# The first MLP product of a hybrid encoder step as a seven-product block scheme too

## The chip, the cores and the metric

The kernel runs on one core of a Trainium2 chip. The metric is the device time of one launch in microseconds (us). Shown are the median of three runs and one profiled execution. TensorE (PE) multiplies, VectorE (DVE), ScalarE (ACT) and GpSimd (POOL) do elementwise work, SyncE (SP) issues most of the loads.

## The reference

One step of a two-layer encoder on 1056 tokens (1024 of a prompt, 32 of a running stream) of width 1024, in fp32. Each layer mixes tokens (layer 0 by causal pooling, layer 1 by differential attention, both beside an attention into 256 memory tokens), projects, and runs an MLP of width 4096:

```python
def sq_relu_mlp(x, w1, w2):
    h = jax.nn.relu(x @ w1)
    return (h * h) @ w2
...
        x = x + jnp.concatenate([t_out, m_out], axis=-1) @ w_out[l]
        x = x + sq_relu_mlp(rmsnorm(x, g_ffn[l]), w_ff1[l], w_ff2[l])
    return rmsnorm(x, g_final), ...
```

`rmsnorm` divides a token by the root of its mean square and multiplies by a gain per channel.

## The kernel before

**Data.** Tokens lie in the free dimension, in three groups g0, g1, g2 of 352 (`GW`); channels lie on partitions, in 8 chunks of 128. An fp32 operand is held as two parts, `hi` (a rounded copy, cast by ScalarE) and `lo` (source minus `hi`, on GpSimd or VectorE). `mm3` (lines 44 to 46) makes one fp32 product of three matmuls: hi·hi, hi·lo, lo·hi. `part` (lines 98, 99) splits a weight tile of 512 columns, `split` (lines 49, 50) a tile of 352.

**PSUM.** In the MLP eight banks: four `xb`, two `mm`, two `dn`. A bank is taken again when VectorE has read what was in it.

**Stages.** Layer 0's mixer (to about 234 us), output projection (to 326), MLP (to 1010), layer 1's mixer (to 1411), projection (to 1504), MLP (to 2213), last stores. `tail` is projection and MLP: the projection goes by three sets of output chunks j, each over all three groups; x gets the result added (line 948), its squares are summed (lines 178, 179), `rstd` (lines 188 to 195: a ones matmul, then ScalarE, then VectorE) makes the scale `rs` of each token, and `take` (lines 208, 209) splits x times the gains. The scale itself is multiplied in only after ff1 (line 1104).

**MLP.** The hidden width is worked through in 16 blocks b of 256, which are two chunks of 128. `ff1(b)` makes six results (two chunks by three groups), each a sum over 8 input chunks, 144 matmuls a block; VectorE makes relu(product) times `rs` (line 1104), ScalarE squares (line 1105). `ff2_pair(b)` already takes g0 and g1 through a 2x2 block product with seven products instead of eight: its weights are four blocks A11 to A22 and four sums S1 to S4, its hidden operands B11 to B22 and T1 to T4; g2 runs plainly. That is 44 products of 3 matmuls, and VectorE adds them to x in 40 evictions (lines 1123 `xb`, 1132 `mm` singles, 1144 plain g2). The last two blocks' second product runs plainly in `ff2_last`.

**What sets the order.** `ff1(b+1)` and `ff2_pair(b)` are woven step by step, three matmuls of each in turn. Splits, weight sums (line 1041, VectorE) and hidden differences (line 1080, GpSimd) are jobs with hand-written places in a count of 48 steps a block (`self.job`). A weight sum may be placed no earlier than the eviction that was last when its job came up (`issue_after(self.last_add...)`). Within such limits a scheduler fixes each engine's list at build time; each engine then runs its own list in order and waits on semaphores. Weights come as raw tiles of 512 KB, three in flight; ten hi/lo pairs are held.

Of the kernel before, what the change touches and what calls it, by code (L numbers as in the profile page):

```python
# [29 lines left out]
NW = 10  # L30
NWB = 14
YOFF = 896
# [3 lines left out]
class Kern:  # L36
# [15 lines left out]
    def weights(self):  # L52
# [14 lines left out]
        for l in range(2):  # L67
            if l:
                for h in range(4):
                    yield t["w_kv"][h], GKV, g  # L70
                    yield t["w_kv"][4 + h], GKV, g
                    yield t["w_in"][8 + h], GA + 8, g
                for h in range(4):
                    yield t["w_in"][12 + h], GA + 8, g
            for j in range(8):
                yield t["w_out"][8 * l + j], None, g
            yield from ((t["w_ff1"][32 * l + i], None, g) for i in range(2))
            yield None

    def raw_tile(self):  # L80
        return self.wpool.tile([128, 8, 128], F32, tag="wraw", name="wraw", bufs=3)

    def weight_load(self):
        if self.wstop:
            return
        w = next(self.wlist, None)
        if w is None:
            self.wstop = True
        else:
            raw = self.raw_tile()  # L90
            self.nc.sync.dma_start(raw.rearrange("p a b -> p (a b)"), w[0])
            self.wraw.append((raw,) + w[1:])

    def part(self, src, eng):

        hi = self.wpool.tile([128, 4, 128], F32R, tag="whi", name="whi", bufs=NW)
        lo = self.wpool.tile([128, 4, 128], F32R, tag="wlo", name="wlo", bufs=NW)
# [4 lines left out]
    def weight_split(self):  # L102
# [5 lines left out]
        raw, gcol, eng = self.wraw.pop(0)  # L108
        if gcol is not None:
            g = self.gains[:, gcol:gcol + 8].unsqueeze(2).broadcast_to([128, 8, 128])  # L110
            nc.gpsimd.tensor_tensor(raw, raw, g, ALU.mult)
        self.wready.append([self.part(raw[:, 4 * a:4 * a + 4], eng) for a in range(2)])
# [13 lines left out]

    def g_dense(self, ps, W, g):
        for c in range(C):
# [4 lines left out]
        self.tick()  # L133
# [78 lines left out]
    def setup(self):  # L212
        nc, t, ctx, tc = self.nc, self.t, self.ctx, self.tc
        self.done = set()
        self.pu, self.pend, self.last_exp = {}, [], None
# [4 lines left out]
        self.wpool = ctx.enter_context(tc.tile_pool(name="wpool", bufs=1))  # L220
        self.xpool = ctx.enter_context(tc.tile_pool(name="xpool", bufs=1))
        self.xh, self.xl, self.rs = [None] * NG, [None] * NG, [None] * NG
        self.acc2 = self.xpool.tile([128, GW], F32, name="acc2")
# [12 lines left out]
    def setup_late(self, b, p):  # L236
# [3 lines left out]
        self.dists = b.tile([128, 288], F32, name="dists")  # L240
        nc.sync.dma_start(self.dists, t["dists"])
        for i in range(0, 1152, 384):
            dt = p.tile([128, 384], F32, tag="os", name="dt", bufs=2)
# [4 lines left out]
        lq = b.tile([128, 388], F32, name="lq")  # L248
# [14 lines left out]
    def mem_load(self, p):  # L263
        self.mx = p.tile([128, C, 256], F32, name="memx")
        self.nc.sync.dma_start(self.mx, self.t["mem"])

    def mem_rstd(self, p):
        self.mr = p.tile([128, 256], F32, name="mr")
# [323 lines left out]
    def mix0(self, U):  # L592
        nc, t = self.nc, self.t
        with self.tc.tile_pool(name="att0", bufs=1, reuse_waits="tile") as p:
# [11 lines left out]
            with self.tc.tile_pool(name="mem", bufs=1, reuse_waits="tile") as mp:  # L606
                wr = p.tile([128, 4, 128], F32, tag="pA3", name="wpr", bufs=2)
                self.wph = mp.tile([128, 4, 128], F32R, name="wph")
                self.wpl = mp.tile([128, 4, 128], F32R, name="wpl")
                nc.sync.dma_start(wr, t["w_pool"])  # L610
                self.split(self.wph, self.wpl, wr)
                self.mem_load(mp)
                self.mix0_drive(p, mp, dd, qq, qs, U)
# [39 lines left out]
    def diff_project(self, h, p, out, smp):  # L653
# [3 lines left out]
        for g in range(NG):  # L657
# [83 lines left out]
    def diff_scores(self, h, pair, p, d, A):  # L741
# [4 lines left out]
        for i in (2 * pair, 2 * pair + 1):  # L746
# [4 lines left out]
            for c in range(2):  # L751
# [12 lines left out]
                if c:  # L764
                    pr = self.pd.tile([128, Wk], F32, tag="p1", name="pr", bufs=1)
# [124 lines left out]
    def mix1(self):  # L890
        self.nq, self.nmk = 4, 1
        with self.tc.tile_pool(name="att1", bufs=1, reuse_waits="tile") as p, \
                self.tc.tile_pool(name="attd", bufs=1, reuse_waits="tile") as self.pd, \
                self.tc.tile_pool(name="tabs", bufs=1, reuse_waits="tile") as tabs:
            dd, qq = {}, {}
            self.qp = p
            self.claim(p, (("q", 1024, self.nq), ("qf", GW, 2), ("st", 16, 4), ("pA3", 1024, 2), ("aTh", 512, 2),
                           ("aTl", 512, 2), ("mkr", 256, 1), ("mk", 512, 1), ("mv", 512, 1), ("os", 512, 2),
                           ("rs_y", 256, 1), ("rs_r", 256, 1), ("sq", 256, 1), ("of", 256, 2)))
# [3 lines left out]
            self.claim(self.pd, (("kst", NT, 1), ("vst", NT, 1), ("ks", 2 * SEQ, 1), ("std", 8, 4), ("pA2", 768, 2),  # L903
                                 ("p1", 1024, 1), ("v", 2 * SEQ, 1)))
            self.setup_late(tabs, p)
# [11 lines left out]
    def tail(self, l):  # L917
        nc, t = self.nc, self.t
        with self.tc.tile_pool(name=f"ff{l}", bufs=1, reuse_waits="tile") as p:
            xin = t["xT"] if l == 0 else self.xscr  # L920
            with ExitStack() as st:
                pad = st.enter_context(self.tc.tile_pool(name=f"pad{l}", bufs=1, reuse_waits="tile"))
                self.claim(pad, (("pad", 4000, 1),))
                po = st.enter_context(self.tc.tile_pool(name=f"out{l}", bufs=1, reuse_waits="tile"))
                o = [po.tile([128, 8, GW], F32, name=f"o{g}") for g in range(NG)]
                for cs in (range(7), range(7, 8)):
                    for g in range(NG):
                        for c in cs:
                            nc.sync.dma_start(o[g][:, c, :], self.oscr[l][c][:, g * GW:(g + 1) * GW])
                for g in range(NG):  # L930
                    self.alloc_x(g)
                    for c in range(8):
                        self.take(o[g][:, c, :], g, c)
                x = [p.tile([128, C, GW], F32, name=f"x{g}") for g in range(NG)]
                acc = [p.tile([128, GW], F32, name=f"acc{g}") for g in range(NG - 1)] + [self.acc2]
                self.claim(p, (("sq", GW, 2),))
                for g in range(NG):
                    nc.sync.dma_start(x[g][:, 0:3], xin[g][:, 0:3])
                for g in range(NG):
                    nc.sync.dma_start(x[g][:, 3:8], xin[g][:, 3:8])  # L940
                for js in ((0, 1, 2), (3, 4, 5), (6, 7)):
                    W = {j: self.weight() for j in js}
                    for g in range(NG):
                        for j in js:
                            k = 3 * g + j
                            ps = (self.xtile if js[0] == 0 and 2 <= k < 6 else self.dntile)()[:, :GW]
                            self.dense(ps, W[j], g)
                            nc.vector.tensor_tensor(x[g][:, j, :], x[g][:, j, :], ps, ALU.add)
                            self.sumsq_add(acc[g], x[g][:, j, :], j == 0, p, eng=nc.gpsimd if j < 6 else None)
                        if js[-1] == 7:  # L950
                            self.alloc_x(g)
                            for c in range(8):
                                self.take(x[g][:, c, :], g, c, GF + 8 * l)
                            self.after(1, lambda g=g: self.rstd(acc[g], D, self.new_rs(g)))
            with self.tc.tile_pool(name=f"h2{l}", bufs=1, reuse_waits="tile") as ph:
                self.ff(l, p, ph, x, acc)
# [5 lines left out]
    def ff(self, l, p, ph, x, acc):  # L962
        self.at, self.jobs, self.ph = -48, [], ph
        self.rawlist = [t for b in range(NWB) for t in (("a", b + 1, 0), ("r", b, 0), ("r", b, 1), ("a", b + 1, 1))]
        self.rawlist += [("a", NB - 1, 0), ("a", NB - 1, 1)] + [("r", NWB + i, k) for i in range(2) for k in range(2)]
        self.raws, self.W1, self.W2, self.H = {}, {}, {}, {}
# [4 lines left out]
        for b in range(NWB, NB):  # L971
            self.plan_last(b)
        for b in range(1, NB):
            for i in range(2):
                at = 48 * (b - 1) + (14 if i else -10)
                self.job(at, lambda b=b, i=i: self.first_part(b, i))
        self.jobs.sort(key=lambda x: x[0])
        self.l = l
        self.W1[0] = [self.weight(), self.weight()]
        for _ in range(3):  # L980
            self.next_raw(l)
        for _ in self.ff1(0):
            self.pos()
        for b in range(NWB):
            two = self.ff2_pair(b, x)
            for k, _ in enumerate(self.ff1(b + 1)):
                next(two, None)
                self.pos()
            for _ in two:
                pass  # L990
# [343 lines left out]
```

## Time and profile before

| | us |
|---|---|
| median of three runs (lowest, highest) | 2225.0 (2223.94, 2226.67) |
| profiled execution, its own time | 2226.33 |
| its span | 2224.6 |
| TensorE busy, matmuls | 2162.5, 13521 |
| VectorE / GpSimd / ScalarE busy | 1314.4 / 1174.6 / 913.8 |
| mean granted TensorE clock | 0.988 |

The profile is of one execution. "L1041 DVE" is an instruction of line 1041 on VectorE; `out<-in` are the program's names, then shapes, count, busy time and mean. In a timeline a row gives start, duration, engine, line, and in brackets how long the engine was idle before and what ended that. Several instructions of a kind in a row are put together (x3).

### The profile page before, as it was taken

The numbers are of one execution on the slowest core, as the hardware profiler recorded it, in microseconds if no ns is written. First come the engines' busy times: TensorE is split into PE (matmuls) and PEld (weight loads), VectorE is DVE, ScalarE is ACT, GpSimd is POOL, SyncE is SP. The second block draws the span as 40 slices with busy tenths as digits, with TensorE's granted clock in tenths as the row PEclk, the third lists the DMA queues.
The fourth block names the chain that finished last, engine by engine and source line by source line (L and its number), as shares of the span: only waits on it lengthen the run. The fifth ranks groups of instructions, "written<-read, shape, count | busy, mean of one in ns | idle before, by whom it ended". The sixth has DMA issues, their size and how long they took to land.

```text
span 2224.6 us, 35342 instructions
## 1 busy us (share of the span) xinstructions
PE 2162.5 (97%) x13521; PEld 2120.0 (95%) x13521; DVE 1314.4 (59%) x2466; ACT 913.8 (41%) x1947; POOL 1174.6 (53%) x1096
## 2 busy tenths in 40 slices
PE   6999999999999999999999999999999999999997
PEld 6898999999999999998999988899999999999997
DVE  8855255566566666647566776235666656665635
ACT  5455353333333333334466766344333333333335
POOL 5225336666666666653433223335666666766653
PEclk9999999999999999999999999999999999999999
DMA  5445401111111111223222214411111111211112
GB/s 190 148 134 171 143 29 38 48 58 48 40 47 58 48 48 38 64 61 134 89 72 58 75 53 126 146 37 39 39 48 58 48 46 40 60 46 48 39 48 79
DMA packets 63642, 158.02 MB, mean 71 GB/s; under 512 B 10608, under 2 KB 30320, under 8 KB 62960
## 3 DMA queue, kind: packets, MB, share of 16 engines
q1 hardware_dynamic: 62176, 152.03, 21.7%
q10 hardware_dynamic: 1296, 3.74, 0.5%
q8 instruction: 106, 1.74, 0.3%
q14 instruction: 64, 0.52, 0.1%
HBM read 125.66 MB, written 25.88 MB: 68 GB/s over the span
## 4 chain that ended last, share of the span: by engine, by line
PE 84%; DVE 5%; ACT 4%; issue 1%; DMA 1%; SPq 0%; DVEq 0%; ACTq 0%
PE dn L44 16%; PE dn L45 16%; PE dn L46 16%; PE mm L44 7%; PE mm L45 7%; PE mm L46 7%; PE xb L44 4%; PE xb L46 4%; PE xb L45 4%; DVE xl L50 1%; PE sc L759 1%; PE mm L801 1%; PE sc L761 1%; PE sc L760 1%; DMA o<-oscr 1%
## 5 line engine op out<-in xcount | busy, mean ns | idle before, releaser
L44 PE MATMUL dn<-xh,whi 128*128 128x352 f32 x2408 | 787.7, 327 | 15.8 <-ACT xh L208 7.6
L45 PE MATMUL dn<-xl,whi 128*128 128x352 f32 x2408 | 779.7, 324 | 1.9 <-DVE xl L209 1.9
L46 PE MATMUL dn<-xh,wlo 128*128 128x352 f32 x2408 | 777.9, 323 | 0.0
L99 POOL TENSOR_TENSOR wlo<-wraw,whi 128x512 fp32r<-128x512 f32 x332 | 434.8, 1317 | 483.6 <-ACT whi L98 483.0
L44 PEld LDWEIGHTS dn<-xh,whi 128*128 128x128 f32 x2408 | 455.4, 189 | 20.2 <-ACT xh L208 7.6
L45 PEld LDWEIGHTS dn<-xl,whi 128*128 128x128 f32 x2408 | 456.0, 189 | 6.1 <-DVE xl L209 3.4
L46 PEld LDWEIGHTS dn<-xh,wlo 128*128 128x128 f32 x2408 | 456.2, 189 | 0.3
L98 ACT CAST whi<-wraw 128x512 fp32r<-128x512 f32 x368 | 223.9, 620 | 542.9 <-PE mm L45 256.3
L1123 DVE TENSOR_TENSOR x<-x,xb 128x352 f32<-128x352 f32 x448 | 233.5, 521 | 172.9 <-PE xb L46 172.8
L44 PE MATMUL mm<-h2h,whi 128*128 128x352 f32 x880 | 284.9, 324 | 0.0
L46 PE MATMUL mm<-h2h,wlo 128*128 128x352 f32 x880 | 283.2, 322 | 0.0
L45 PE MATMUL mm<-h2l,whi 128*128 128x352 f32 x880 | 282.7, 321 | 0.0
L1132 DVE TENSOR_TENSOR x<-x,mm 128x352 f32<-128x352 f32 x448 | 222.6, 518 | 85.1 <-PE mm L46 84.9
L50 POOL TENSOR_TENSOR h2l<-hid,h2h 128x352 fp32r<-128x352 f32 x164 | 154.8, 951 | 103.2 <-ACT h2h L49 99.2
L1144 DVE TENSOR_TENSOR x<-x,mm 128x352 f32<-128x352 f32 x224 | 116.3, 519 | 148.9 <-PE mm L46 148.9
L1105 ACT ACTIVATE hid<-hid 128x352 f32<-128x352 f32 x192 | 95.3, 496 | 230.9 <-DVE hid L1104 229.0
L99 POOL TENSOR_TENSOR wlo<-ws,whi 128x512 fp32r<-128x512 f32 x112 | 168.1, 1521 | 37.5 <-ACT whi L98 20.0
L1104 DVE SCALAR_TENSOR_TENSOR hid<-dn,rs 128x352 f32<-128x352 f32 x192 | 100.1, 521 | 132.6 <-PE dn L46 130.8
L45 PEld LDWEIGHTS mm<-h2l,whi 128*128 128x128 f32 x880 | 165.5, 188 | 0.4
L44 PEld LDWEIGHTS mm<-h2h,whi 128*128 128x128 f32 x880 | 165.3, 188 | 0.4
L46 PEld LDWEIGHTS mm<-h2h,wlo 128*128 128x128 f32 x880 | 165.4, 188 | 0.0
L44 PE MATMUL xb<-h2h,whi 128*128 128x352 f32 x448 | 144.5, 322 | 0.0
(243 smaller groups left out, 3416.1 us busy)
## 6 DMA issues: line engine op xcount, KB each, us to landing
wraw<-in_w_ff SPq DMA_DIRECT2D x128, 512.0 KB, 3.6
o<-oscr SPq DMA_DIRECT2D x48, 176.0 KB, 3.6
wraw<-in_w_in SPq DMA_DIRECT2D x16, 512.0 KB, 4.1
wraw<-in_w_mem SPq DMA_DIRECT2D x16, 512.0 KB, 3.8
wraw<-in_w_out SPq DMA_DIRECT2D x16, 512.0 KB, 3.9
x<-in_xT SPq DMA_DIRECT2D x12, 352.0 KB, 7.6
xscr<-x SPq DMA_DIRECT2D x3, 1408.0 KB, 4.7
out_y<-x SPq DMA_DIRECT2D x24, 176.0 KB, 1.8
```

What stands on the lines that cost most here:

```text
L44: mm(ps, lhsT=ah, rhs=bh, start=first, stop=False, skip_group_check=more)
L45: mm(ps, lhsT=ah, rhs=bl, start=False, stop=False, skip_group_check=more)
L46: mm(ps, lhsT=al, rhs=bh, start=False, stop=last, skip_group_check=more)
L50: (lo_eng or self.nc.vector).tensor_tensor(lo, src, hi.bitcast(F32), ALU.subtract)
L98: self.nc.scalar.copy(hi, src)
L99: eng.tensor_tensor(lo, src, hi.bitcast(F32), ALU.subtract)
L759: nc.tensor.matmul(o, lhsT=self.slid[:, h, :], rhs=self.dtab[:, y:y + n], start=True, stop=False)
L1104: nc.vector.scalar_tensor_tensor(h, ps, 0.0, self.rs[g], ALU.max, ALU.mult)
L1105: nc.scalar.activation(h, h, AF.Square)
L1123: add(xj, xj, X[j], ALU.add)
L1132: add(xj, xj, ps, ALU.add)
L1144: self.last_add = add(xj, xj, ps, ALU.add)
```

## The change

The first MLP product of g0 and g1 becomes the same kind of seven-product scheme, block by block: 44 steps of three matmuls instead of 48, 132 matmuls a block instead of 144. Relu needs the finished result, so the scheme's operands must be normalised tokens: x times gain times `rs` is made before (line 1004 of the changed kernel), and from it the operands B11, B21, B22 and T1 to T4 once a layer (`operands0`, `operands1`; g2 in `operands2`), each split into hi and lo. ff1's weights get S1 to S4 in each block too: eight parts a block instead of four, and four more sums on VectorE (line 1148). Partial sums p1, p4, u3 live in freed tiles. Relu and square are two ScalarE instructions (lines 1188, 1189).

In ff2 the splits of its S weights move from GpSimd to VectorE (line 102); its products come in another order and there are 44 evictions (line 1319), since the chain S3·T3 has two targets. ff2 lags ff1 by 66 steps of 44 a block. The output projection keeps six banks open over chunks 0 to 6 and does g2 before chunks j3 to j7 of g0, g1, g2. Raw weight tiles are 256 KB, six in flight; eight hi/lo pairs are held. Groups are finished in the order 2, 0, 1 (`ORDER`), and pools and the tables of layer 1's mixer are set up in another order (`setup_late`).

VectorE in the woven MLP. `mm`, `xb` and `dn` are PSUM banks, `x_2604` to `x_2606` (before) and `x_2657` to `x_2659` (after) the three groups. Before, among the plain products of g2:

```order
L1144 TENSOR_TENSOR x_2606<-x_2606,mm 128x352
L1041 TENSOR_TENSOR ws<-wraw 128x512
L1144 TENSOR_TENSOR x_2606<-x_2606,mm 128x352
L1041 TENSOR_TENSOR ws<-ws,wraw 128x512
L1144 TENSOR_TENSOR x_2606<-x_2606,mm 128x352
L1041 TENSOR_TENSOR ws<-wraw 128x512
L1104 SCALAR_TENSOR_TENSOR hid<-dn,rs_3399 128x352
L1144 TENSOR_TENSOR x_2606<-x_2606,mm 128x352
L1041 TENSOR_TENSOR ws<-wraw,ws 128x512
```

Now, at the end of the plain products of g2 and through the singles A22·T4 (`x_2657`) and S4·B22 (`x_2658`):

```order
L1319 TENSOR_TENSOR x_2659<-x_2659,mm 128x352 x2
L102 TENSOR_TENSOR wlo<-ws,whi 128x512
L1319 TENSOR_TENSOR x_2657<-x_2657,mm 128x352
L1148 TENSOR_TENSOR ws<-wraw 128x512
L1319 TENSOR_TENSOR x_2657<-x_2657,mm 128x352
L1148 TENSOR_TENSOR ws<-ws,wraw 128x512
L1319 TENSOR_TENSOR x_2657<-x_2657,mm 128x352
L1148 TENSOR_TENSOR ws<-wraw 128x512
L1319 TENSOR_TENSOR x_2657<-x_2657,mm 128x352
L1319 TENSOR_TENSOR x_2658<-x_2658,mm 128x352
L1148 TENSOR_TENSOR ws<-wraw,ws 128x512
```

These four sums are those of ff1's weights; ff2's own four still stand among the plain products, further up. In the step from the projection into ff1, VectorE's list now ends thus (T_3391 and T_3392 are T3 and T4, the sums those of block 0, `rs_3690` the scale of g2):

```order
L53 TENSOR_TENSOR T_3391<-xf,T_3391 128x352 x2
L964 TENSOR_TENSOR x_2659<-x_2659,mm 128x352
L1051 TENSOR_TENSOR xf<-xf,t_3487 128x352
L1051 TENSOR_TENSOR xf<-xf,t_3489 128x352
L184 TENSOR_TENSOR acc_2662<-acc_2662,sq 128x352
L53 TENSOR_TENSOR T_3392<-xf,T_3392 128x352 x2
L1148 TENSOR_TENSOR ws<-wraw 128x512
L1258 TENSOR_TENSOR b_3682<-p_3667,dn 128x352
L1148 TENSOR_TENSOR ws<-ws,wraw 128x512
L1148 TENSOR_TENSOR ws<-wraw 128x512
L1148 TENSOR_TENSOR ws<-wraw,ws 128x512
L198 SCALAR_TENSOR_TENSOR rs_3690<-xb,rs_3690 128x352
```

The weight sums of block 0 stand behind the last operand, T4; before, this place held only casts' `lo` parts and the scales. The core of the diff:

```diff
-NW = 10
+NW = 8
+NRAW = 6
+STEPS = 44
+ORDER = (2, 0, 1)
...
-                for js in ((0, 1, 2), (3, 4, 5), (6, 7)):
-                    W = {j: self.weight() for j in js}
-                    for g in range(NG):
-                        for j in js:
...
+        for g in range(2):
+            for j in range(3, 8):
+                ps = self.bank()
+                self.dense(ps, W[j], g)
+                added(g, j, ps)
+            if g == 0:
+                self.after(1, lambda: self.operands0(l, sp, po, x[0], acc[0]))
+        more = self.operands1(l, sp, p, po, x[1], acc[1])
+        for j in range(3, 8):
+            ps = self.bank()
+            self.dense(ps, W[j], 2)
+            added(2, j, ps)
+            next(more, None)
...
+        for c in range(4):
+            b12.append(self.norm(l, 1, x, c, po))
+            v(b11[c], b12[c], b11[c], ALU.subtract)
+            self.put("T1", c, b11[c], c % 2)
...
         for b in range(NB):
-            self.plan_hidden(b)
+            self.plan_weights("a", b, STEPS * b, (("A11", -8), ("A12", -2), ("A21", 8), ("A22", 12), ("S2", 20),
+                                                  ("S3", 24), ("S1", 28), ("S4", 32)))
         for b in range(NWB):
-            self.plan_pair(b)
+            at = STEPS * (b + 1) + 22
+            self.plan_weights("r", b, at, (("A12", -8), ("A11", -4), ("A21", 8), ("A22", 10), ("S4", 20), ("S2", 24),
+                                           ("S1", 28), ("S3", 32)))
...
-            with self.tc.issue_after(self.last_add.ins):
-                nc.vector.tensor_tensor(s, x, y, op)
+            with self.tc.issue_after(self.last_add.ins) if self.last_add else ExitStack():
+                nc.vector.tensor_tensor(S[k], x, y, op)
...
         def part(k):
+            src = S.pop(int(k[1])) if k[0] == "S" else raw(("A11", "A12", "A21", "A22").index(k))
+            self.A[kind, b, k] = self.part(src, nc.vector if k[0] == "S" and kind == "r" else g)
...
+        for k in range(4):
+            self.job(at + 12 + 2 * k, lambda k=k: add(k + 1))
...
+    def ff1(self, b):
+        yield from self.plain(b, 1)
+        yield from self.one(b, "A11", "B11")
+        p1 = self.role("p1")
+        nc.scalar.copy(p1, self.ps)
+        yield from self.one(b, "A12", "B21")
+        h = self.role("B11")
+        add(h, p1, self.ps, ALU.add)
+        self.hidden(b, "B11", h, h)
...
+    def ff1_first(self):
+        yield from self.one(0, "A11", "B11")
...
+        yield from self.one(0, "A12", "B21")
...
+        yield from self.one(0, "S4", "B22")
...
+        yield from self.one(0, "S1", "T1")
...
+        yield from single("A12", "B21", (0, 0))
+        yield from plain(0, "A11", "A12")
+        yield from chain("A11", "B11", (0, 0), first=True)
+        yield from plain(1, "A21", "A22")
+        yield from single("A22", "T4", (0, 1))
+        yield from single("S4", "B22", (1, 0))
+        yield from chain("S2", "T2", (1, 0))
+        yield from single("S1", "T1", (1, 1), (1, 0))
+        yield from chain("S3", "T3", (1, 1), (0, 1))
```

More of the change, by code (lines that the diff above doesn't have):

```diff
@@ L125, in dense, with g_dense @@
             pass
-    def g_dense(self, ps, W, g):
-        for c in range(C):
+    def g_dense(self, ps, W, g, chunks=range(C)):
+        for c in chunks:
             hi, lo = W[c // 4]
@@ L988, in ff @@
+            self.plan_hidden(b, at)
+        self.plan_last(sp)
+        self.jobs.sort(key=lambda x: x[0])
+        third = self.operands2(l, ph, x[2], acc[2])
+        for _ in self.ff1_first():
+            self.pos()
+            if self.at > 8:
+                next(third, None)
+        second = self.second(x)
+        for b in range(1, NB):
+            for _ in self.ff1(b):
                 self.pos()
-            for _ in two:
-                pass
-        for _ in self.ff1(NB - 1):
-            self.pos()
+                if self.at > STEPS + 22:
+                    next(second, None)
@@ L993, in ff @@
+        for _ in second:
+            pass
         while self.jobs:
@@ L995, in ff, with second @@
         self.wstop = False
-        self.ff2_last(l, p, x, acc)
+        self.ff2_last(l, p, x)
+    def second(self, x):
+        for b in range(NWB):
+            yield from self.ff2_pair(b, x)
     def job(self, at, fn):
@@ L1095, in ff1, with raw @@
[L1095 to L1106 removed]
+        def raw(k):
+            return self.raws[kind, b, k]
@@ new lines, in part @@
+        def part(k):
+            src = S.pop(int(k[1])) if k[0] == "S" else raw(("A11", "A12", "A21", "A22").index(k))
+            self.A[kind, b, k] = self.part(src, nc.vector if k[0] == "S" and kind == "r" else g)
+        if kind == "a" and b == 0:
+            part("A11")
+            part("A12")
+            a22 = []
+            for k in (1, 2, 3):
+                add(k)
+            a21 = raw(2), raw(3)
+            add(4)
+            for k in ("S4", "S1", "S2", "S3"):
+                part(k)
+            self.A["a", 0, "A22"] = self.part(a21[1], g)
+            self.A["a", 0, "A21"] = self.part(a21[0], g)
+            return
@@ new lines, in hidden, with steps @@
+    def hidden(self, b, k, src, h=None):
+        h = h or self.role(k)
+        self.nc.scalar.activation(h, src, AF.Relu)
+        self.nc.scalar.activation(h, h, AF.Square)
+        self.H[b][k] = h
+    def steps(self, ps, b, a, x, first=True, last=True):
+        hi, lo = self.A["a", b, a]
+        for c in range(4):
+            if isinstance(x, int):
+                bh, bl = self.xh[2][:, 4 * x + c, :], self.xl[2][:, 4 * x + c, :]
+            else:
+                bh, bl = self.X[x][:, 0, c, :], self.X[x][:, 1, c, :]
+            self.mm3(ps, hi[:, c, :], lo[:, c, :], bh, bl, first and c == 0, last and c == 3)
+            yield
@@ L1130, in single, with plain @@
                 for g, u in to:
-                    xj = x[g][:, j + 4 * u, :]
-                    add(xj, xj, ps, ALU.add)
-        yield from chain("A11", "B11", 0, 0, first=True)
-        yield from single("A12", "B21", (0, 0))
-        for u, a1, a2 in ((0, "A11", "A12"), (1, "A21", "A22")):
+                    add(g, j, u, ps)
+        def plain(u, a1, a2):
             for j in range(4):
@@ L1208, in x_rstd @@
         nc = self.nc
-        acc = [p.tile([128, GW], F32, name=f"acc{g}{i}") for i in range(2)]
+        acc = [p.tile([128, GW], F32, tag=f"acc{i}", name=f"acc{g}{i}", bufs=2) for i in range(2)]
         for c in range(C):
```

506 lines of the change are left out of this document (313 added, 193 removed).

## The prediction

> **What bounds the kernel now.** I read the page first, then the table of windows, then VectorE's and GpSimd's timelines inside one steady stretch of the MLP. From the page, the engines' busy time and the head of the chain of waits:
>
> ```profile
> PE 2162.5 (97%) x13521; PEld 2120.0 (95%) x13521; DVE 1314.4 (59%) x2466; ACT 913.8 (41%) x1947; POOL 1174.6 (53%) x1096
> PE 84%; DVE 5%; ACT 4%; issue 1%; DMA 1%; SPq 0%; DVEq 0%; ACTq 0%
> ```
>
> The windows (per stretch: length, then busy time and instructions of PE, PEld, DVE, ACT, POOL, the granted clock, DMA share, GB/s):
>
> ```profile
> 400.00:900.00 500.00, 500.00 (x3138) 500.00 (x3138) 307.00 (x565) 161.29 (x310) 327.47 (x286) 1.00 0.16 49
> 1580.00:2080.00 500.00, 500.00 (x3139) 500.00 (x3138) 306.93 (x566) 160.44 (x308) 326.81 (x286) 1.00 0.16 50
> 486.00:529.00 43.00, 43.00 (x271) 43.00 (x270) 26.37 (x50) 14.07 (x27) 27.30 (x24) 1.00 0.17 50
> 310.00:330.00 20.00, 19.61 (x118) 18.70 (x117) 17.70 (x33) 15.39 (x34) 5.46 (x4) 1.00 0.00 0
> 1034.00:1064.00 30.00, 23.64 (x118) 23.17 (x119) 22.15 (x34) 10.62 (x24) 16.22 (x16) 0.83 0.43 146
> ```
>
> In both MLPs TensorE is never idle: 500 us for 3138 matmuls, 0.1593 us each, at full clock. The step from the output projection into the MLP (310 to 330) loses only 0.4 us. The whole kernel is TensorE's list of matmuls plus some 60 us of gaps elsewhere; a removed matmul is worth its 0.159 us as long as VectorE (61% busy in the steady stretch) and GpSimd (65%) still answer in time.
>
> **What is removed.** The first MLP product falls from 144 to 132 matmuls in each of 16 blocks and two layers: 16 x 2 x 12 = 384 matmuls, 384 x 0.1593 = **61.2 us**. A woven pair of an ff1 block and an ff2 block falls from 276 matmuls (43.97 us) to 264 (42.06 us), so 28 pairs hold 1.91 x 28 = 53.5 us of it; the rest lies in blocks without a partner.
>
> **What is added in a pair.** VectorE gets four more evictions or sums, four more weight sums (line 1148) and the four `lo` splits of the S weights (line 102). Its durations, from the timelines of VectorE and of GpSimd:
>
> ```profile
> 488.71 0.52 DVE L1144 TENSOR_TENSOR x<-x,mm 128x352 f32<-128x352 f32 x1 [1.37 <-PE mm L46]
> 489.14 1.29 DVE L1041 TENSOR_TENSOR ws<-wraw 128x512 f32<-128x512 f32 x1
> 491.07 0.72 DVE L1041 TENSOR_TENSOR ws<-ws,wraw 128x512 f32<-128x512 f32 x1
> 492.98 1.43 DVE L1041 TENSOR_TENSOR ws<-wraw 128x512 f32<-128x512 f32 x1
> ...
> 495.20 0.92 DVE L1041 TENSOR_TENSOR ws<-wraw,ws 128x512 f32<-128x512 f32 x1
> 498.30 0.52 DVE L1144 TENSOR_TENSOR x<-x,mm 128x352 f32<-128x352 f32 x1 [1.40 <-PE mm L46]
> 500.21 0.52 DVE L1144 TENSOR_TENSOR x<-x,mm 128x352 f32<-128x352 f32 x1 [1.40 <-PE mm L46]
> ...
> 506.90 2.86 DVE L1132 TENSOR_TENSOR x<-x,mm 128x352 f32<-128x352 f32 x6 [0.43 <-PE mm L46]
> ```
> ```profile
> 488.03 1.85 POOL L50 TENSOR_TENSOR h2l<-hid,h2h 128x352 fp32r<-128x352 f32 x2 [2.21 <-ACT h2h L49]
> 489.84 1.40 POOL L50 TENSOR_TENSOR h2l<-hs,h2h 128x352 fp32r<-128x352 f32 x1
> 492.58 4.70 POOL L99 TENSOR_TENSOR wlo<-ws,whi 128x512 fp32r<-128x512 f32 x3 [1.33 <-PE mm L46]
> 497.24 0.95 POOL L1080 TENSOR_TENSOR hs<-hid 128x352 f32<-128x352 f32 x1
> ```
> ```profile
> L1041 DVE TENSOR_TENSOR ws<-wraw 128x512 f32<-128x512 f32 x56 | 76.6, 1367 | 0.0
> L1041 DVE TENSOR_TENSOR ws<-wraw,ws 128x512 f32<-128x512 f32 x28 | 25.9, 925 | 0.0
> L1041 DVE TENSOR_TENSOR ws<-ws,wraw 128x512 f32<-128x512 f32 x28 | 20.5, 731 | 0.0
> L99 DVE TENSOR_TENSOR wlo<-wraw,whi 128x512 fp32r<-128x512 f32 x36 | 26.4, 744 | 16.4 <-ACT whi L98 16.0
> L99 POOL TENSOR_TENSOR wlo<-wraw,whi 128x512 fp32r<-128x512 f32 x332 | 434.8, 1317 | 483.6 <-ACT whi L98 483.0
> L98 ACT CAST whi<-wraw 128x512 fp32r<-128x512 f32 x368 | 223.9, 620 | 542.9 <-PE mm L45 256.3
> ```
>
> An eviction from PSUM takes 0.52 and leaves VectorE free after 0.43 (488.71 to 489.14). A weight sum of the same form takes 0.72 where GpSimd soon falls idle (491.07; GpSimd's split ends at 491.24) and 1.29 or 1.43 where a GpSimd operation is under way (489.14, 492.98). In these rows the sum ends about 0.57 after the GpSimd operation under way does (489.84 to 490.43; 491.24 to 491.79), and the GpSimd operation behind it is stretched (1.40 for one that takes 0.95).
>
> The Trainium skill, page "SBUF — State Buffer", section "Who interferes with whom", has a rule that speaks against this change: a VectorE operation with two SBUF inputs and a GpSimd operation that reads SBUF share a port, and the second to issue waits until the first has ended. The rows agree with it. By the rule, in an unbroken row of GpSimd work, each of the new sums would wait out a GpSimd split less the eviction ahead of it (estimate: 1.29 - 0.44 + 0.57 = 1.42), and the stall below would lie near its upper bound.
>
> *VectorE's load of a pair*: 44 ff2 evictions and 6 ff1 sums at about 0.46 make 23; eight weight sums at 1.10 (mean of the three groups above) 8.8; four splits at 0.74 to 1.3, 3 to 5. Together 35 to 37 of 42.06 us, 85%, where before it was 26.4 of 43. GpSimd has 12 weight splits at 1.3, nine hidden splits, four subtractions and a sum at 0.95: 29 of 42. Both fit on average. The question is where the work stands.
>
> *Its place.* Before, the four sums stand between evictions of the plain products, one every 1.92 us (498.30, 500.21). Now four sums (the r weights) still stand there, but the other four (the a weights) stand between the evictions of the single products A22·T4, one every 6 x 0.1593 = 0.956 us. There are two `mm` banks, so a product takes the bank of the one 1.91 us before it. From TensorE's timeline, one such product:
>
> ```profile
> 506.23 0.32 PE L44 MATMUL mm<-h2h,whi 128*128 128x352 f32 x1
> ...
> 506.55 0.32 PE L46 MATMUL mm<-h2h,wlo 128*128 128x352 f32 x1
> ```
>
> Its eviction starts at 506.90, 0.67 after its start, and takes 0.52; so VectorE may be 0.70 us late, and what is beyond holds TensorE. With the group means in program order: 0.44 + 1.37 - 0.956 = 0.85 late, a stall of 0.15; then 0.44 + 0.73 - 0.956 = 0.21 more, stall 0.21; then 0.85 more, stall 0.85; the fourth sum has an interval without a sum ahead of it and adds nothing. Sum 1.2 us. The S splits stand directly before these singles and between the plain evictions (1.92 apart); at 0.74 they fit, at 1.25 they hand on 0.3 to 1 us. GpSimd's list runs through here without a gap (four subtractions, then weight and hidden splits in turn), so I take **1.6 us a pair**: 28 x 1.6 = 45 us. Bounds: every sum at 0.72 and every split at 0.7, nothing is more than 0.7 late, 0 to 0.25 us, 0 to 7 us in all; every sum at 1.43 (492.98) and the splits at 1.1, three stalls of 0.9 and one of 0.4 from the sums and 1 from the splits, about 4 us, 112 us in all.
>
> **What is added at the step into the MLP** (twice). From VectorE's timeline of the old step and of the kernel's start, GpSimd's at both, and TensorE's after a gap at 228:
>
> ```profile
> 306.64 0.52 DVE L948 TENSOR_TENSOR x<-x,dn 128x352 f32<-128x352 f32 x1 [2.14 <-PE dn L46]
> 308.70 3.06 DVE L209 SCALAR_TENSOR_TENSOR xl<-x,gains,xh 128x352 fp32r<-128x352 f32 x6
> 313.97 0.52 DVE L195 TENSOR_TENSOR rs<-rs,rs_y 128x352 f32<-128x352 f32 x1
> 20.50 8.83 DVE L209 SCALAR_TENSOR_TENSOR xl<-x,gains,xh 128x352 fp32r<-128x352 f32 x8
> ```
> ```profile
> 319.78 5.50 POOL L99 TENSOR_TENSOR wlo<-wraw,whi 128x512 fp32r<-128x512 f32 x4 [18.04 <-ACT whi L98]
> 20.10 1.27 POOL L1218 TENSOR_TENSOR acc<-acc,sqp 128x352 f32<-128x352 f32 x1
> ```
> ```profile
> 228.60 0.50 PE L44 MATMUL dn<-xh,whi 128*128 128x352 f32 x1
> 230.87 0.32 PE L46 MATMUL dn<-xh,wlo 128*128 128x352 f32 x1
> ```
>
> Count from the end of the last projection product of group 1. TensorE then has five products of group 2 (120 matmuls, 19.1 us) and A11·B11, A12·B21 (24, 3.8 us): work until 22.9. Next is S4·B22, and S4 is a weight sum which stands on VectorE behind all of T1 to T4. The scale of group 1 is there 7.8 us after the last eviction (306.64 to 314.49). Then come 34 SBUF operations of 352 columns (8 norms, 10 splits, 12 differences, 4 sums of squares), four evictions, four weight sums. At 0.51 an operation (308.70, GpSimd idle) this is 17.3 + 1.8 + 3.3 = 22.4, done at 30.2; at a third of the way to 1.10 (20.50, GpSimd busy) 24 + 1.8 + 4.5, done at 38. ScalarE's cast (0.62) and GpSimd's `lo` (1.3) follow: the third matmul of S4·B22 can run at 32 to 40. TensorE idles 9 to 17 us, and then runs at the half clock first: 8 matmuls in 2.27 us (228.60 to 230.87) for 1.27, 1 us more. I take 13 each, **26 us** for both; the least is 0 to 4 (if the norms are spread better than their order suggests), the most 34. Cover for the old step was that VectorE needed only casts and `lo` of the tokens, 8 operations a group.
>
> **Smaller terms.** The relu and square (two ScalarE operations a result for one VectorE and one ScalarE) and copies of p1, p4 lie on ScalarE, 33% busy in a pair: nothing. Half-tile loads double the DMA issues on SP but not the bytes, at a share of 0.16: nothing, and 2 us if a queue held them. At the entry of the last ff2 GpSimd has more splits to catch up: 3 us (0 to 6). At the entry of mixer 1, VectorE is held 1.70 us for a table and TensorE idles 6.4 of 30 us:
>
> ```profile
> 1052.37 2.03 DVE L245 CAST dtab<-dt 128x384 fp32r<-128x384 f32 x1 [1.70 <-DMA dt<-in_dtab]
> ```
>
> The table's load now stands ahead of other claims on its pool, and group 2 is finished first; I take 4 us back (0 to 8). The output projection's reordering removes no matmul; its six open banks wait less for the last heads: 0 (2 either way).
>
> **Sum.** The profiled execution took 2226.3, the median of the runs is 2225.0, 1.3 lower. 2226.3 - 61.2 + 45 + 26 + 3 - 4 = 2235, 2234 as a median.
>
> **Rivals.** *(A) VectorE keeps up in the pairs.* The sums meet GpSimd's gaps (13 of 42 us) and cost 0.3 us a pair, 8 us; the step costs 10 each. 2225 - 61 + 8 + 20 - 1 = **2191**. For it: 491.07 at 0.72, and means of 85% load. Against it: 1.37 as the mean of 56 sums. *(B) Half the stall.* 0.8 a pair (22 us), 11 a step, 2225 - 61 + 22 + 22 - 1 = **2207**, faster by less than 1%. *(C) The port locks everywhere.* Also the slower side, one mechanism: the S splits, new on VectorE, alternate with GpSimd's splits at 1.25, so VectorE enters the singles already 0.7 late and each later sum is paid in full; from a split of about 1.1 on this decides. 3.5 us a pair, 98 us: 2225 - 61 + 98 + 30 - 1 = **2291**. For it: 1.43 and 1.10 above; against it: the mean of 36 splits, 0.744. *(D) The step costs nothing and the pairs nothing*: 2225 - 61 = **2164**; the order of the rows speaks against it.
>
> **Chances.** The forecast 0.42 (its own range 2218 to 2250), A 0.22, B 0.17, C 0.15, D 0.04. The range over all: 2184 to 2275. What a measurement of this kernel can tell from no change is about 0.2%, 2220.5 to 2229.5. Slower: 0.30 of the forecast and C, 0.45. The same: 0.10 of the forecast and 0.03 of B, 0.13. Faster: A, D, the rest of B and 0.02 of the forecast, 0.42.
>
> **What would show it.** In the windows of the MLP TensorE's busy time should fall below the length of the stretch, by some 1.6 us in each 43.6, with the idle time released by VectorE evictions from `mm` at line 1319 behind line 1148; about 264 matmuls per 43 to 44 us. VectorE's busy share there should be near 85%. Sums at line 1148 between `mm` evictions should show 1.2 to 1.4 us. At about 335 and again near 1510 there should be one gap of TensorE of 9 to 17 us, ended by the `lo` of S4 and followed by matmuls at 0.29. If the pairs show no idle time, A or D is right; if TensorE's matmul count is not 13137 the first term is wrong; if VectorE's splits at line 102 are over 1.1 us, C is.

## The result, and the profile after

The changed kernel takes 2277.7 us (median of four runs, 2269.0 to 2278.8) where the kernel before took 2225.3: a ratio of 1.0227, interval 1.0201 to 1.0253. It is slower by 52 us. The forecast was slower, 2234; the time lies 3 us outside the range given. The profiled execution took 2278.8, its span is 2277.0. The page's busy line, and the head of its chain of waits:

```profile
PE 2159.1 (95%) x13137; PEld 2074.8 (91%) x13137; DVE 1614.5 (71%) x2890; ACT 1108.9 (49%) x2357; POOL 1304.6 (57%) x1192
PE 73%; DVE 17%; issue 3%; ACT 3%; DMA 2%; POOL 1%; SPq 0%; DVEq 0%; ACTq 0%; POOLq 0%
```

The 384 matmuls are gone (13521 to 13137), yet the span is longer, and VectorE's share of the chain has grown from 5% to 17%. The table of windows of the changed kernel, first a steady stretch, then the step into the MLP:

```profile
500.00:900.00 400.00, 392.80 (x2376) 380.59 (x2375) 314.53 (x558) 179.33 (x351) 276.13 (x235) 1.00 0.15 48
300.00:360.00 60.00, 40.37 (x212) 37.80 (x212) 56.48 (x73) 27.38 (x58) 41.29 (x31) 0.80 0.08 25
```

TensorE seems 98% busy in the steady stretch. Count the matmuls instead: at 0.1593 us each, 2376 of them are 378.5 of 400 us, so 5% of the time is lost, of which the busy time shows a third. The period of a pair is to be read from one instruction that comes once a block (VectorE's timeline):

```profile
523.04 0.51 DVE L1234 TENSOR_TENSOR u<-p,dn 128x352 f32<-128x352 f32 x1
...
656.61 0.51 DVE L1234 TENSOR_TENSOR u<-p,dn 128x352 f32<-128x352 f32 x1
```

Three periods in 133.57 us, 44.52 each, for 264 matmuls that are worth 42.06: 2.46 us lost a pair, 69 us in 28 pairs. (Over the 13 periods of layer 0's MLP the mean is 44.49.)

**A ledger by stages.** The end of the projection in layer 0 is 325.6 before and 318.2 after (322.04, where the first gap begins, less the 24 matmuls of the first two products). The first eviction of the last ff2 is at 988.0 and 1009.7; the answers for the lines that hold it:

```profile
L1165 DVE TENSOR_TENSOR x<-x,mm x24: 508/515/522, 988.0 to 2209.7; 128x352 f32<-128x352 f32 x24
```
```profile
L1401 DVE TENSOR_TENSOR x<-x,mm x24: 505/514/522, 1009.7 to 2262.0; 128x352 f32<-128x352 f32 x24
```

| stage | before, us | after, us | difference |
|---|---|---|---|
| start to the end of layer 0's projection | 325.6 | 318.2 | -7.4 |
| layer 0's MLP up to its last ff2 | 662.4 | 691.5 | +29.1 |
| last ff2, mixer 1, projection 1 | 515.7 | 517.1 | +1.4 |
| layer 1's MLP up to its last ff2 | 662.3 | 691.6 | +29.3 |
| last ff2, output | 58.5 | 58.6 | +0.1 |

The first row is of one execution: in the profiles of the runs below whose program is the same up to there, the stage ends between 320.2 and 323.2, so its gain is 2.4 to 7.4 us. All of the loss lies in the two MLPs. In each, 192 matmuls less are -30.6 us, 14 pairs at 2.46 are +34.4, and what is left, 25 us, is the step from the projection into the MLP. The second window above says the same: the kernel before runs 369 matmuls in these 60 us, the changed one 212, and 157 matmuls are 25.0 us.

**The place in the pair.** VectorE's timeline at the singles A22·T4, GpSimd's beside it, and TensorE's:

```profile
622.67 1.39 DVE L102 TENSOR_TENSOR wlo<-ws,whi 128x512 fp32r<-128x512 f32 x1
623.98 0.51 DVE L1319 TENSOR_TENSOR x<-x,mm 128x352 f32<-128x352 f32 x1
624.41 1.00 DVE L1148 TENSOR_TENSOR ws<-wraw 128x512 f32<-128x512 f32 x1
625.33 0.51 DVE L1319 TENSOR_TENSOR x<-x,mm 128x352 f32<-128x352 f32 x1
625.77 0.99 DVE L1148 TENSOR_TENSOR ws<-ws,wraw 128x512 f32<-128x512 f32 x1
626.68 0.51 DVE L1319 TENSOR_TENSOR x<-x,mm 128x352 f32<-128x352 f32 x1
627.11 0.99 DVE L1148 TENSOR_TENSOR ws<-wraw 128x512 f32<-128x512 f32 x1
628.03 0.94 DVE L1319 TENSOR_TENSOR x<-x,mm 128x352 f32<-128x352 f32 x2
628.89 1.82 DVE L1148 TENSOR_TENSOR ws<-wraw,ws 128x512 f32<-128x512 f32 x1
630.64 0.94 DVE L1319 TENSOR_TENSOR x<-x,mm 128x352 f32<-128x352 f32 x2
```
```profile
624.82 2.74 POOL L1297 TENSOR_TENSOR t<-b,t 128x352 f32<-128x352 f32 x2
627.51 1.40 POOL L53 TENSOR_TENSOR h2l<-g,h2h 128x352 fp32r<-128x352 f32 x1
628.88 1.28 POOL L102 TENSOR_TENSOR wlo<-wraw,whi 128x512 fp32r<-128x512 f32 x1
```
```profile
627.33 0.40 PE L47 MATMUL mm<-h2h,whi 128*128 128x352 f32 x1 [0.21 <-DVE x L1319]
627.57 0.33 PE L48 MATMUL mm<-h2l,whi 128*128 128x352 f32 x1
...
631.20 0.43 PE L47 MATMUL mm<-h2h,whi 128*128 128x352 f32 x1 [0.43 <-DVE x L1319]
```

The first three sums take 1.0 each beside GpSimd operations on 352 columns (0.95 undisturbed, 1.37 to 1.40 here), and the fourth takes 1.82 beside a split of 1.28. TensorE's products there start 0.10, 0.39, 0.48, 0.30, 0.10, 0.59 and 0.10 later than 0.956 after the one ahead: 2.06 of the 2.46 us. The first 0.10 follows VectorE's own split of 622.67, the next four (1.27) the first three sums, the last two (0.69) the fourth. The remaining 0.40 is spread, and taken up below.

**The step.** TensorE's timeline in both layers, each row a gap of TensorE:

```profile
332.09 1.54 PE L193 MATMUL xb<-acc,ones 128*128 128x352 f32 x2 [10.05 <-DVE acc L184]
336.76 0.66 PE L47 MATMUL dn<-B,whi 128*128 128x352 f32 x1 [3.13 <-ACT whi L101]
338.31 0.66 PE L49 MATMUL dn<-B,wlo 128*128 128x352 f32 x1 [0.59 <-POOL wlo L102]
352.14 0.66 PE L47 MATMUL dn<-T,whi 128*128 128x352 f32 x1 [5.80 <-ACT b L1266]
...
1540.69 1.54 PE L193 MATMUL xb<-acc,ones 128*128 128x352 f32 x2 [10.04 <-DVE acc L184]
```

There is the forecast gap before S4·B22, in pieces of 10, 3 and 0.6 us. The first piece does not end with S4: group 2's ones matmul (line 193) stands ahead of S4·B22 in TensorE's list, and waits for group 2's last sum of squares, which VectorE has among the operands. The other two end with S4's cast and `lo`. And there is a second gap that was not forecast, 5.8 us, ended by a copy on ScalarE, which takes a product out of one of the two `dn` banks. The row's 0.66 us is a matmul at half the clock; the clock falls in both gaps, and behind them 13 and 12 matmuls follow each other at 0.29 us instead of 0.16, which with the slow restarts costs some 4 us a layer.

### The profile page after: what moved, and what is told of

Its sections match the earlier page's. It is cut to its first block, busy times and chain, and to the rows that moved or that the text cites. A ratio compares the mean times of both kernels' runs of the same rounds, so it can differ in the third digit from the quotient of the medians.

```text
span 2277.0 us, 36104 instructions
## 1 busy us (share of the span) xinstructions
PE 2159.1 (95%) x13137; PEld 2074.8 (91%) x13137; DVE 1614.5 (71%) x2890; ACT 1108.9 (49%) x2357; POOL 1304.6 (57%) x1192
## 4 chain that ended last, share of the span: by engine, by line
PE 73%; DVE 17%; issue 3%; ACT 3%; DMA 2%; POOL 1%; SPq 0%; DVEq 0%; ACTq 0%; POOLq 0%
PE dn L47 12%; PE dn L49 12%; PE dn L48 12%; PE mm L47 7%; PE mm L48 7%; PE mm L49 7%; DVE ws L1148 5%; PE xb L47 4%; PE xb L49 4%; PE xb L48 4%; DVE x L1319 3%; DVE xf L1004 1%; PE sc L764 1%; PE sc L766 1%; PE sc L765 1%
## 5 line engine op out<-in xcount | busy, mean ns | idle before, releaser
L47 PE MATMUL dn<-xh,whi 128*128 128x352 f32 x1160 | 384.8, 332 | 14.6 <-ACT xh L213 8.5
L48 PE MATMUL dn<-xl,whi 128*128 128x352 f32 x1160 | 378.8, 327 | 0.7 <-DVE xl L214 0.7
L49 PE MATMUL dn<-xh,wlo 128*128 128x352 f32 x1160 | 377.9, 326 | 0.0
L47 PEld LDWEIGHTS dn<-xh,whi 128*128 128x128 f32 x1160 | 221.0, 191 | 19.2 <-ACT xh L213 9.0
L48 PEld LDWEIGHTS dn<-xl,whi 128*128 128x128 f32 x1160 | 221.6, 191 | 4.6 <-DVE xl L214 2.9
L49 PEld LDWEIGHTS dn<-xh,wlo 128*128 128x128 f32 x1160 | 221.0, 191 | 0.3
L101 ACT CAST whi<-ws 128x512 fp32r<-128x512 f32 x240 | 142.8, 619 | 118.8 <-PE xb L48 86.0
L47 PE MATMUL dn<-T,whi 128*128 128x352 f32 x512 | 168.1, 328 | 11.9 <-ACT b L1266 11.6
L49 PE MATMUL dn<-T,wlo 128*128 128x352 f32 x512 | 167.3, 327 | 0.0
L48 PE MATMUL dn<-T,whi 128*128 128x352 f32 x512 | 167.3, 327 | 0.0
L53 POOL TENSOR_TENSOR h2l<-t,h2h 128x352 fp32r<-128x352 f32 x112 | 117.7, 1051 | 50.8 <-ACT h2h L52 50.8
```

Source lines behind the costliest of these rows:

```text
L47: mm(ps, lhsT=ah, rhs=bh, start=first, stop=False, skip_group_check=more)
L48: mm(ps, lhsT=ah, rhs=bl, start=False, stop=False, skip_group_check=more)
L49: mm(ps, lhsT=al, rhs=bh, start=False, stop=last, skip_group_check=more)
L53: (lo_eng or self.nc.vector).tensor_tensor(lo, src, hi.bitcast(F32), ALU.subtract)
L101: self.nc.scalar.copy(hi, src)
```

## The experiments

All are run beside the kernel before; 2277.7 is the changed kernel. Theory P is the forecast's for the pair: it is the place of ff1's sums.

**ff1's sums left out** (blocks 1 to 15; ScalarE copies a raw tile in the sum's place):

```diff
-                nc.vector.tensor_tensor(S[k], x, y, op)
+                if kind == "a" and b:
+                    nc.scalar.copy(S[k], x)
+                else:
+                    nc.vector.tensor_tensor(S[k], x, y, op)
```

> Leaves out ff1's weight sums in blocks 1 to 15: ScalarE copies one raw tile into each sum's place, so VectorE loses four operations a pair and every other row keeps its place. Theory P (place: the sums between the A22T4 singles hold the mm banks): the pair's period, 44.5 us in the changed kernel, falls to 42.2 to 42.5, the whole to 2277.7 - 28 x 2.1 = about 2219. Rival S (the four S splits, new on VectorE, cause the stall): the period stays above 43.8, the whole above 2258. The step from the projection into the MLP stays as it is under both.

Measured 2224.9 (ratio to before 0.9992, 0.9983 to 1.0001), 53 us less than the changed kernel. The period is 42.47 us (mean of 13, VectorE's line 1237), as P said; TensorE waits for no eviction in the steady stretch:

```profile
500.00:900.00 400.00, 400.00 (x2488) 400.00 (x2487) 286.87 (x548) 205.61 (x402) 274.28 (x245) 1.00 0.15 48
```

P stands: the four S splits are still on VectorE here. Left are 42.47 - 42.06 = 0.4 us a pair without any wait: TensorE's matmuls follow each other at 0.1608 us (400 / 2488) where it was 0.1593. The same 0.1608 shows in the changed kernel outside of the stalls, and 0.1601 to 0.1609 in the profiles of all the experiments. Whether that belongs to the kernel or to these executions stays open; it is worth some 12 us.

**The S splits back on GpSimd:**

```diff
-            self.A[kind, b, k] = self.part(src, nc.vector if k[0] == "S" and kind == "r" else g)
+            self.A[kind, b, k] = self.part(src, g)
```

> Undoes one part: the lo splits of ff2's S weights go back from VectorE to GpSimd. Theory P: only the carry of the split that stands right before the singles goes, 0.3 to 0.5 us a pair, and GpSimd has more work beside the sums: 2264 to 2278. Rival S: most of the 2.47 us goes: about 2220.

Measured 2292.6 (1.0294, 1.0276 to 1.0311): worse by 15, outside what either theory said. VectorE's timeline names a new wait:

```profile
634.41 0.51 DVE L1319 TENSOR_TENSOR x<-x,mm 128x352 f32<-128x352 f32 x1
635.66 1.41 DVE L1148 TENSOR_TENSOR ws<-wraw,ws 128x512 f32<-128x512 f32 x1 [0.75 <-POOL wlo L102]
```

There are four tiles for the sums, and now the fourth sum waits for GpSimd to have split an older one; the evictions stand behind it. So on VectorE these splits are worth 15 us as long as ff1's sums stand there too. Rival S falls by the run before, in which the splits stay and no wait is left; this run, with a wait of its own, could not have shown it.

**ff1's sums on GpSimd:**

```diff
-                nc.vector.tensor_tensor(S[k], x, y, op)
+                (g if kind == "a" and b else nc.vector).tensor_tensor(S[k], x, y, op)
```

> Moves ff1's four weight sums of blocks 1 to 15 from VectorE to GpSimd. Theory P: the stall at the singles goes, period 42.2 to 42.8, the whole 2217 to 2230, with GpSimd at 80%. Rival G (GpSimd becomes the bound: 29 + 5 of 42 us, its list in order, parts late): TensorE waits for lo parts instead, period over 44, 2265 or more.

Measured 2230.4 (1.0018, 1.0009 to 1.0028), 47 us less, with all of the work done. GpSimd is 81% busy and no bound in the pair:

```profile
500.00:900.00 400.00, 400.00 (x2494) 399.23 (x2493) 289.90 (x548) 186.26 (x367) 324.51 (x284) 1.00 0.16 50
```

The 5.5 us by which it stays above the run without the sums lie in the step: the second gap is 9.29 us here and 5.83 there, in each layer.

**Group 2's norms later** (`if self.at > 20` for `> 8`):

> Group 2's scale and norms are put after step 20 of the first MLP block instead of step 8, nothing else. Theory Q (ScalarE's and VectorE's lists: group 2's norms stand ahead of the copies that free the two dn banks, the second gap of 5.8 us and its half clock): that gap goes, 6 to 9 us a layer, 2260 to 2266. Rival M (the gap only moves: the plain products of group 2 wait for the same norms): within 3 us of 2277.7.

Measured 2275.6 (1.0226, 1.0209 to 1.0243). This says nothing on Q: the scheduler put the norms and the ones matmul where they had been, and the trace has the same gaps, 10.03, 3.12 and 5.83 us. A place in the program is not yet a place in the list.

**Block 0's sums before group 1's operands:**

```diff
+        self.first_sums(l, po)
         more = self.operands1(l, sp, p, po, x[1], acc[1])
```

(The loads of the raw tiles move there with them.)

> Block 0's four weight sums are made before the operands of group 1 (on VectorE, about 300 us, from tiles that are in by then), not behind T4; nothing else. Theory of the prediction (S4 is late because its sum stands last): the 10 us gap goes, 2277.7 - 2 x 10 = 2258. Rival L (TensorE's ones matmul for group 2's scale stands ahead of S4 in its list and waits for VectorE's last sum of squares): the gap of 10 stays, only the 3.1 us behind it go, 2269 to 2273.

Measured 2285.7 (1.0270, 1.0250 to 1.0290): no gain, 8 us worse as medians. The gap of 10 us before S4·B22 is still there, but another row ends it, and a new gap of 3.45 us stands ahead of it (TensorE's timeline):

```profile
340.19 0.66 PE L47 MATMUL dn<-B,whi 128*128 128x352 f32 x1 [9.86 <-ACT p L1269]
...
363.93 0.66 PE L47 MATMUL dn<-T,whi 128*128 128x352 f32 x1 [9.25 <-DVE p L1282]
```

S4 is there now, and the product waits for a bank: the copy of the first product (line 1269) stands behind casts of the operands in ScalarE's list, and the sum of line 1282 behind group 2's norms in VectorE's. Neither the late sum nor rival L alone is the cause.

**The same, with group 2's ones matmul pinned late:**

```diff
+        with self.tc.issue_after(self.pe_last.ins):
             self.rstd(acc, D, self.new_rs(2))
```

(In the program the norms also come after step 18 instead of 8.)

> As the run with early sums, and group 2's ones matmul is pinned behind the fifth product of block 0. Theory L: TensorE goes on with S4, S1 and S2 as their operands come; the step loses 10 to 14 us instead of 24 a layer, 2250 to 2258. Rival D (VectorE's list of operands sets it whatever TensorE's order): within 4 us of the run with early sums.

Measured 2287.7 (1.0271, 1.0257 to 1.0285): within 4 us of the run before, as D said. The gaps are 9.86 (the same copy) and 9.20 us. L falls.

**All operand work on VectorE** (`c % 2` dropped from every `put`, `g if c % 2 else v` replaced by `v`):

> All splits and differences of the operands are put on VectorE (14 more operations of 352 a layer for groups 0 and 1 and 4 for group 2), GpSimd idles there; nothing else. Port theory (the two engines take turns, so a GpSimd operation of 0.95 costs VectorE more than doing it itself at 0.44): T4 is ready 2 to 4 us earlier and group 2's norms take 7 instead of 14 us: 2256 to 2262. Rival W (work sharing helps): 18 x 0.44 = 8 us a layer later, 2293.

Measured 2272.8 (1.0215, 1.0197 to 1.0233): 5 us less as medians, with intervals that overlap those of the changed kernel, so it is not settled by time. It is not the 2256 to 2262 of the port theory either. The rows are clear against W. TensorE's first gap, which ends with VectorE's last sum of squares, ends 5.9 us earlier:

```profile
326.18 1.54 PE L193 MATMUL xb<-acc,ones 128*128 128x352 f32 x2 [4.28 <-DVE acc L184]
...
334.25 0.66 PE L47 MATMUL dn<-B,whi 128*128 128x352 f32 x1 [6.52 <-ACT whi L101]
```

VectorE does 18 operations more for groups 0 and 1 (14 splits, four differences), and gets there earlier; but S4, last in its list, gains only 2.5 us (334.25 for 336.76), and the wait for it grows from 3.13 to 6.52.

**Together:** ff1's sums on GpSimd (block 1's behind the last hidden difference), early sums, the pin, operands on VectorE.

> Sums of ff1 on GpSimd, block 0's sums early, group 2's scale pinned late, operands on VectorE. If the two causes (place of the sums in the pair, the step's lists) are what the change lost, it is below the kernel before: 2230 - 2 x (14 to 20) = 2190 to 2202. If the step's loss is something else (the two dn banks, held by copies that stand behind casts in ScalarE's list): 2212 to 2222.

Measured 2230.3 (1.0016, 1.0007 to 1.0025), no better than the sums on GpSimd alone and above both cases. The step has three gaps left, 3.91, 9.05 and 8.67 us, and all end with a read of a `dn` bank. The first, at 326.36, is the eviction of a product of the projection (line 964); the rows of the other two:

```profile
341.05 0.66 PE L47 MATMUL dn<-T,whi 128*128 128x352 f32 x1 [9.05 <-ACT b L1278]
...
359.61 0.63 PE L47 MATMUL dn<-xh,whi 128*128 128x352 f32 x1 [8.67 <-DVE u L1289]
```

**Eight banks for the first block.** The `xb` and `mm` banks stand empty until ff2 begins. First alone in the changed kernel:

```diff
-        ps = self.dntile()[:, :GW]
+        ps = self.bank() if b == 0 else self.dntile()[:, :GW]
```

> The changed kernel, but the first block's nine products take the eight PSUM banks by turns, which stand empty until ff2 begins, instead of the two dn banks; nothing else. Theory B (the second gap of 5.8 us comes of the two dn banks, held by copies and sums that stand behind operands and norms in the lists of ScalarE and VectorE): that gap and its half clock go, 6 to 8 us a layer, 2262 to 2266. Rival V (the products wait for VectorE's operands and norms themselves): within 3 us of 2277.7.

Measured 2279.1 (1.0232, 1.0215 to 1.0250), nothing gained, which is the time of rival V. The second gap is gone, as B said, but the first is now one of 14.39 us, ended by the cast of S4, and behind it the plain products of group 2 wait for its norms and splits, up to 1.15 us at a time:

```profile
340.40 0.66 PE L47 MATMUL xb<-B,whi 128*128 128x352 f32 x1 [14.39 <-ACT whi L101]
...
357.15 0.43 PE L48 MATMUL mm<-xl,whi 128*128 128x352 f32 x1 [1.15 <-DVE xl L53]
```

So a `dn` bank ended the second gap, but did not by itself cost it: without the bank, TensorE waits for the norms that stood ahead of the bank's readers.

Then on top of everything together:

> As the run with everything together (2230), and the first block's products on eight banks. Theory B: the two gaps of 9 us a layer, each ended by a copy or a sum out of a dn bank, go; what stays is the wait for T2 to T4 and for group 2's norms, about 8 us a layer: 2200 to 2210. Rival V: 2225 or more.

Measured 2218.8 (0.9972, 0.9960 to 0.9984): 11 us below the run without the banks, 59 below the changed kernel, and 0.3% faster than the kernel before. It misses B's 2200 to 2210. What is left of the step is the wait for the operands themselves and for group 2's norms:

```profile
336.70 1.54 PE L193 MATMUL xb<-acc,ones 128*128 128x352 f32 x2 [4.96 <-DVE acc L184]
...
346.79 0.42 PE L47 MATMUL mm<-xh,whi 128*128 128x352 f32 x1 [3.69 <-ACT xh L52]
```

These waits are most of what the step cost. In its window the changed kernel runs 212 matmuls and the kernel before 369; here it is 253:

```profile
300.00:360.00 60.00, 46.78 (x253) 42.84 (x252) 52.04 (x87) 31.60 (x69) 24.65 (x18) 0.91 0.06 18
```

So 116 matmuls are missing against the kernel before, 18.5 us, and a gap of 2.54 follows at 366 us: some 21 of the 25 us of a step are still lost. VectorE is busy for 28.8 of the 29 us from 310 to 339 us.

Last, the same without the early sums:

> As the run before, but block 0's weight sums stay behind T4, so that no weight split of GpSimd's runs beside VectorE's operands. Theory B with the port: T1 to T4 are ready earlier by the five or six operations that were stretched to 1.6 us (5 us), but S4, first of them, comes only after T4: within 5 us of the other, 2202 to 2215. Rival V: 2225 or more.

Measured 2225.4 (0.9995, 0.9986 to 1.0003): 7 us worse than with them, a gap of 11.89 us that ends with S4's cast. With banks free, the early sums do pay.

So the step has several holds in a row: group 2's ones matmul, S4's late sum, the two banks, and behind them VectorE's list of operands and norms. Taking one away lets the next one hold TensorE for nearly as long: the sums alone and the banks alone gave nothing, on top of everything else the banks gave 11 us and the early sums 7. With all of the edits together some 21 us a step remain. That these are the amount of VectorE's work, and no longer its order, is argued from its busy time and not shown; no run makes that work smaller.

## Why the prediction was right or wrong

- **61.2 us removed:** right in count (13137). Its worth is less, by some 12 us in the pairs, if the spacing of 0.1608 belongs to the change, which stays open.
- **Place, not load, costs in the pair:** right. Taking the four ff1 sums away, or to GpSimd, gives 53 and 47 us; moving S splits gives none. Rivals A, B and D are out: the pairs do not keep up, and half the stall is too little. C's sign did show, though not in the mean of 0.896: of the four S splits of a pair the last, right ahead of the singles, takes about 1.4 in 26 of 28 pairs, and VectorE enters the singles 0.8 us late, as C had it (an eviction at 623.98 for a product begun at 622.51, where 0.67 later is usual). C's price did not come, 2.46 for 3.5, since three of the four sums took 1.0. The time lies between the forecast's own range, to 2250, and C's 2291, which the range over all had left out.
- **1.6 us a pair, 45 in all, was too small:** this term failed, measured 2.46 and 69. The step most at fault is "the fourth sum has an interval without a sum ahead of it and adds nothing": here it meets a GpSimd split of 1.28, takes 1.82 and costs TensorE 0.59 + 0.10 = 0.69. Another 0.40 is the wider spacing, which no term held. The 0.4 that was left for the S splits shows as only 0.10 of direct stall. That the first three sums' stall came out right, 1.2 forecast and 1.27 measured (0.39 + 0.48 + 0.30 + 0.10), is luck: they were costed at 1.37, 0.73 and 1.37 from a VectorE that is not late, and took 1.00, 0.99 and 0.99 from one that was.
- **The rule that the Trainium skill gives** ("SBUF — State Buffer", "Who interferes with whom"), that the second operation waits for the first to end: this trace agrees. GpSimd's split of 628.88 ends at about 630.16, and the sum issued at 628.89 ends at 630.71, 0.55 later. The estimate by the rule, nearly the upper bound, leaned the right way, though three of the four met operations that take 0.95 undisturbed, and not 1.29.
- **13 us a step, 26 in all, was too small:** the second term that failed, measured 25 and 51. The first gap was right in place and size (10.05 + 3.13 + 0.59 for 9 to 17); its cause only in part, since the 10.05 end with group 2's sum of squares and not with S4. What failed is that the count ended at S4·B22. VectorE's list goes on behind S4's sum with eight norms and four splits of group 2, which the count put at nothing; the readers of the two `dn` banks stand behind them, and the 5.8 us come of it. With the banks free the norms themselves held TensorE, and nothing was gained. The half clock was counted once, for 8 matmuls and 1 us; it fell twice, for 25 matmuls and some 4 us.
- **The smaller terms:** the projection's new order was costed at 0 and the first stage is 7.4 us shorter in this execution, 2.4 to 5.4 in others; the entry of mixer 1, 4 us back, and GpSimd's backlog, 3 us, came to a loss of 1.4 together in the stage that holds both. Half tiles, relu and copies did not show as waits in the pair.
- Sum: 45 to 69 and 26 to 51 (25.3 and 25.5) is 49 us, less about 5 in the small ones: 2234 + 44 = 2278.

## What to carry to other kernels

An average load (85% forecast, 79% measured in the steady stretch) says nothing about a queue that runs in order: ask how late the engine may be where each operation stands, here 0.70 us between singles that share two banks, and cost an operation by what the neighbour engine does at that very place; a mean over four splits hid the one that counted. When a gap's cause is found, go on along the lists to what would hold next (bank, operand, scale): here several holds stood in a row, and neither the early sums nor the banks alone gave anything. Where the busy time says 98%, count instructions.

## What the runs showed of the hardware

- A VectorE operation with two SBUF inputs and a GpSimd operation take turns: a weight sum took 0.68 alone (332.83) and 1.82 behind a GpSimd split. Giving GpSimd part of the operand work did not help VectorE: with 18 operations more, its last sum of squares came 5.9 us earlier.
- A product that waited for its bank pays more than the wait: its second matmul starts 0.24 to 0.27 us after the first, where 0.16 is usual (627.33 and 627.57).
